# An encoder's last output rows: a spectrum's split moved into its step, the last product in two banks, the last store in quarters

## The chip, the cores and the metric

The kernel runs on one core of a Trainium2 chip. A core has a matrix engine (TensorE, PE in the profile; its weight loads are listed as PEld), a vector engine (VectorE, DVE), a scalar engine (ScalarE, ACT), GpSimd (POOL) and a sync engine (SyncE, SP) that issues transfers; transfers are also issued from the queues of ACT and POOL, and 16 DMA engines carry them all. Matrix products are accumulated in PSUM, in banks of 128 partitions by 512 fp32 columns; everything else on the chip lies in SBUF. The metric is the device time of one execution in microseconds (us), as the median of several runs.

## The reference: what is computed

Two sequences, of 2048 and of 512 positions with 1024 channels each, go through an encoder trunk of two layers and a final norm:

```
x = x + (banded_gqa(rmsnorm(x) @ w_in) * silu(gate)) @ w_out           # layer 0
h = rmsnorm(x)                                                          # layer 1
hg = h.reshape(b, s, 4, 256)
f = fft.fftn(hg, axes=(positions, group channels), norm="ortho").real
x = x + (f * silu(h @ w_gate)) @ w_fout
y = x * rsqrt(mean(x * x) + 1e-6) * final_norm                          # final RMSNorm
```

All is fp32. The two outputs are y of the two sequences. The change concerns the end of the second layer and the final norm of the last rows.

## The kernel before

**Precision.** An fp32 product is computed as three products in a faster format: each operand is split into a high part (a cast on ACT, `ACT.copy`) and a low part (the difference, a subtraction on DVE), and `matmul3` (lines 92 to 95) multiplies high by high, high by low and low by high. So each product of a 128-row tile with a K of 512 is 4 times 3 = 12 matmuls. Nearly all matmuls have line 95 in the profile and are told apart by their tiles.

**The Fourier layer.** The transform over 2048 positions is 16 by 128. Real and imaginary parts of the 16 "spectra" k1 are made by butterflies on DVE (`pm`, a sum and a difference of 128 by 1024 each, shown at line 1184); only k1 = 0 to 8 are transformed, since each k1 from 1 to 7 gives two tiles of 128 output rows, those of k1 and of 16 - k1. The function `position` (line 1330) transforms one spectrum: for each of two halves of the channels it takes the split operands (`halves_of`, lines 1316 to 1326: for the real and the imaginary part a cast on ACT at line 1323 and a subtraction on DVE at line 1324, 128 by 512 each), runs the products A and B on TensorE, and combines them on ACT and DVE (lines 1354 to 1361) into two tiles u, which are multiplied by the gates (line 1364). The split operands lie in tiles of the tag hT, of which there are eight.

**The output product.** `finish` (line 1384) multiplies u, turned, by the output weights and adds the residual rows, which `residual` loads from DRAM (line 1381). It then calls `normed` (line 1373): sum of squares on ACT (`sumsq`, line 979), the mean on DVE and the power of -1/2 on GpSimd (`inv_rms`, lines 86 to 90), one scaling of 128 by 1024 on DVE (line 1376) and a store issued from SP (line 1377). For the spectra 6, 1, 7, 3, 5 the class `Outs` (line 1397) takes the place of `finish`: both tiles of a spectrum are multiplied together, in seven products of 12 matmuls with sums of weights (T1, T2, T3, N4) and sums of operands (S1 to S4) instead of eight products. Its method `products` (line 1450) accumulates in the tiles W, Z and X, of which three banks (tag acc) serve, shared with the accumulators of `finish`; it adds each to the residual rows xa and xb with the function `add` (line 1457), and runs the next spectrum's `position` between its products.

**Around the sixth spectrum.** The tables T1, T2, T3, N4 (four loads of 512 KB each, line 1505) and many tiles of the butterflies share 16 buffers of the tag R. The real and imaginary parts of spectra 7, 3 and 5 are stored to DRAM (line 1656, issued from ACT) and read back later, which frees their buffers. The code first makes the butterflies up to g3r and g5r, then splits both halves of the sixth spectrum (line 1651), then makes the last butterfly (g5s and g3s, line 1652), then issues the six stores, then transforms the sixth spectrum with the operands made earlier.

**The tail.** In the last call of `products`, for spectrum 5, the last product (A[1, 1] with N4) goes into a bank of its own, Vo. The second half of the row's columns (512 to 1023) is complete before it, so its squares are summed early. After the product come the add, the square of columns 0 to 511, the sum of both, mean, power, and a scaling and a store for each half of the columns, one issued from SP and one from ACT.

**What sets the order.** Tile, the framework, plans the order of each engine's instructions: those that come first in the program go first where the plan finds them ready, by its own costs. An edge written with `after(ins, anchor)` fixes the order of two instructions of one engine. Each engine and each queue carries out its list in order; a load that needs a buffer waits at the head of its queue until the buffer's last reader or writer is done.

Of the kernel before, what the change touches and what calls it, by code (L numbers as in the profile page):

```python
# [9 lines left out]
F32 = mybir.dt.float32  # L10
# [9 lines left out]
P = 128  # L20
D = 1024
# [21 lines left out]
def encoder(  # L43
# [33 lines left out]
    def bank(name):  # L77
        return banks[-1].tile([P, 512], F32, tag="bank", name=name)
# [854 lines left out]
    def fourier_phase(tail):  # L933
        with ExitStack() as es:
# [15 lines left out]
            def zt(name):  # L950
                return right([P, D], F32, name)
# [27 lines left out]
            def sumsq(src, name):  # L979
                ss = main.tile([P, 8], F32, tag="ss", bufs=2, name=f"ss{name}")  # L980
                junk = fp.tile([P, 512], F32, tag="c12", bufs=1, name=f"jk{name}").bitcast(BF16)
                ACT.activation(junk, src, AF.Square, accum_out=ss[:, 0:1])
                return inv_rms(ss, 1, f"inv{name}")
# [413 lines left out]
            class Outs:  # L1397
# [52 lines left out]
                def products(self, hooks, last=False):  # L1450
# [25 lines left out]
                    normed(xa, self.us[0][1])  # L1476
                    prod(W, S[3], ft["T3"], four, False)
                    add(xb, 1, W)
                    if last:
                        ss = main.tile([P, 8], F32, tag="ss", bufs=2, name="ssl")  # L1480
                        junk = fp.tile([P, 512], F32, tag="c12", bufs=1, name="jkl").bitcast(BF16)
                        ACT.activation(junk[:, :512], xb[:, q[1]], AF.Square, accum_out=ss[:, 1:2])
                    if last:

                        add(xb, 0, W)
                        W = bank(f"Vo{self.n}")
                    prod(W, A[1, 1], ft["N4"], four, last)
                    add(xb, 0, W)
                    if not last:
                        normed(xb, self.us[1][1])  # L1490
                        return
                    ACT.activation(junk[:, :512], xb[:, q[0]], AF.Square, accum_out=ss[:, 0:1])
                    DVE.tensor_tensor(ss[:, 0:1], ss[:, 0:1], ss[:, 1:2], ALU.add)
                    inv = inv_rms(ss, 1, "invl")
                    for half in range(2):
                        hs = q[half]
                        DVE.scalar_tensor_tensor(xb[:, hs], xb[:, hs], inv[:, 0:1], gfb[:, hs], ALU.mult, ALU.mult)
                        (SP, ACT)[half].dma_start(out_rows(self.us[1][1])[:, hs], xb[:, hs])
# [152 lines left out]
            p6 = [halves_of("p6", *G[6], hf) for hf in range(2)]  # L1651
# [149 lines left out]
```

## Time and profile before

| | us |
|---|---|
| median of 3 runs | 1583.85 (1583.34 to 1585.53) |
| the profiled execution | 1584.07 |
| its span, first to last instruction | 1582.1 |
| TensorE busy in it | 1569.5 (99%) |
| VectorE busy in it | 1151.0 (73%) |
| mean TensorE clock granted | 0.999 of full speed |

A row of the timeline reads: start (us from the first instruction), duration, engine, line of the kernel, operation, output tile <- input tiles, shapes, and xN where N like ones in a row were merged; in brackets the idle time before it and what ended it. "PE W L95 x24" in the chain is a stretch of time with its start and length. A row of a group reads: line, engine, operation, tiles, shapes, count, then the busy time in us, the mean duration of one in ns, the idle time before them. A row of the DMA issues ends with the size in KB and the time from issue to landing in us. A row of the waits ends with the total in us, the number of waits and the longest. SPq and ACTq are the queues of SP and ACT.

### The profile page before, as it was taken

To read this page: it belongs to the slowest core of one execution; us is meant where nothing else is said; L and a number is where in the kernel's file an instruction comes from. 1 tells how busy PE (TensorE), PEld (TensorE's weight loads), DVE (VectorE), ACT (ScalarE), POOL (GpSimd) and SP (SyncE) were. 2 spreads that over 40 slices of the span, in tenths; PEclk is the share of its full clock that TensorE was granted. 3 is DMA by queue.
4 is the path that set the end of the run, shared out by engine and by line. 5 is a ranking of instruction groups with operands and counts; after the bars stand their busy time and mean duration, and the time that the engine had idled before them with its cause. 6 is when DMAs were issued, how large, how long until landed. Compare 5 with 4: busy or idle time off the path is not lost.

```text
span 1582.1 us, 27442 instructions
## 1 busy us (share of the span) xinstructions
PE 1569.5 (99%) x9743; PEld 1320.8 (83%) x9743; DVE 1151.0 (73%) x2785; ACT 874.5 (55%) x2089; POOL 446.5 (28%) x613
## 2 busy tenths in 40 slices
PE   9999999999999999999999999999999999999998
PEld 7888888888888888988888888888888888887886
DVE  6888656877447886378764577669778878988896
ACT  6688535776246784267752576646555554343342
POOL 2475642421404314024222242223112111011110
PEclk9999999999999999999999999999999999999999
DMA  7598695575856567655659566675567469548752
GB/s 293 200 332 290 227 359 210 207 262 201 295 205 224 205 234 276 216 215 214 257 165 329 208 221 232 236 262 196 196 207 258 175 223 410 183 167 318 264 203 80
DMA packets 101445, 373.89 MB, mean 236 GB/s; under 512 B 12236, under 2 KB 22476, under 8 KB 83901
## 3 DMA queue, kind: packets, MB, share of 16 engines
q1 hardware_dynamic: 82572, 297.91, 52.7%
q0 software_dynamic: 16400, 70.04, 11.4%
q10 hardware_dynamic: 2336, 4.20, 0.7%
q8 instruction: 77, 1.26, 0.3%
q14 instruction: 60, 0.48, 0.1%
HBM read 280.84 MB, written 91.26 MB: 235 GB/s over the span
## 4 chain that ended last, share of the span: by engine, by line
PE 95%; DVE 2%; DMA 1%; issue 0%; ACT 0%; POOL 0%; SPq 0%; DVEq 0%; POOLq 0%; ACTq 0%
PE gp L95 14%; PE qp L95 14%; PE spt L95 11%; PE op L95 7%; PE W L95 6%; PE av L557 6%; PE spt L472 6%; PE fo L95 5%; PE vp L95 3%; PE Z L95 3%; PE Wo L95 3%; PE pt L531 3%; PE Zo L95 2%; PE z L95 2%; PE X L95 2%; PE z L1079 1%
## 5 line engine op out<-in xcount | busy, mean ns | idle before, releaser
L95 PE MATMUL gp<-h,wg 128*128 128x512 f32 x960 | 237.6, 395 | 0.0
L95 PE MATMUL qp<-h,wq 128*128 128x512 f32 x960 | 237.3, 396 | 0.0
L491 DVE CUSTOM_DVE_ANT_0 S<-spt,b 128x385 f32<-128x385 f32 (+1 forms) x320 | 156.3, 527 | 105.1 <-PE spt L472 68.1
L95 PEld LDWEIGHTS gp<-h,wg 128*128 128x128 f32 x960 | 174.9, 188 | 37.2 <-issue 1.0
L95 PEld LDWEIGHTS qp<-h,wq 128*128 128x128 f32 x960 | 174.9, 188 | 36.7 <-issue 0.2
L499 ACT ACTIVATE S<-S 128x385 f32<-128x385 f32 (+1 forms) x320 | 188.8, 596 | 19.7 <-DVE S L491 19.5
L539 ACT CAST pts<-pt 128x384 fp32r<-128x384 f32 (+1 forms) x240 | 100.5, 457 | 168.2 <-PE pt L531 158.6
L540 DVE TENSOR_TENSOR pts<-pt,pts 128x384 fp32r<-128x384 f32 (+1 forms) x240 | 114.3, 519 | 23.3 <-ACT pts L539 22.2
L95 PE MATMUL spt<-wo,uT 128*128 128x512 f32 x480 | 120.4, 391 | 0.0
L581 POOL TENSOR_TENSOR uT<-o,uT 128x256 fp32r<-128x256 f32 x75 | 55.5, 739 | 229.3 <-ACT uT L580 229.2
L95 PE MATMUL op<-wo,uT 128*128 128x512 f32 x480 | 118.9, 391 | 0.0
L472 PE MATMUL spt<-kwin,qab 64*128 64x384 f32 (+1 forms) x960 | 118.4, 352 | 0.0
L557 PEld LDWEIGHTS av<-pts,v 128*128 128x128 f32 x576 | 101.4, 188 | 18.8
L95 PE MATMUL fo<-wo,tTu 128*128 128x512 f32 x480 | 115.7, 392 | 0.3 <-ACT wo L1556 0.3
L557 PE MATMUL av<-pts,v 128*128 128x512 f32 (+1 forms) x576 | 115.7, 341 | 0.0
L95 PEld LDWEIGHTS op<-wo,uT 128*128 128x128 f32 x480 | 89.3, 188 | 18.5
L95 PEld LDWEIGHTS spt<-wo,uT 128*128 128x128 f32 x480 | 89.1, 188 | 18.4
L95 PEld LDWEIGHTS fo<-wo,tTu 128*128 128x128 f32 x480 | 88.3, 188 | 17.6 <-ACT wo L1556 0.7
L511 DVE TENSOR_SCALAR S<-S 128x384 f32<-128x384 f32 (+1 forms) x192 | 96.0, 500 | 6.8
L472 PEld LDWEIGHTS spt<-kwin,qab 64*128 64x128 f32 x960 | 74.6, 186 | 28.2 <-issue 26.4
L577 POOL TENSOR_TENSOR o<-o,s 128x256 f32<-128x256 f32 x75 | 55.3, 737 | 135.1 <-DVE o L575 134.7
L531 PEld LDWEIGHTS pt<-ident,S 64*128 64x128 f32 x1328 | 78.4, 138 | 4.0 <-issue 1.8
(322 smaller groups left out, 3190.9 us busy)
## 6 DMA issues: line engine op xcount, KB each, us to landing
wo<-wsd SPq DMA_DIRECT2D x32, 1024.0 KB, 4.9
wq<-wsd SPq DMA_DIRECT2D x31, 1024.0 KB, 7.4
wg<-wsd SPq DMA_DIRECT2D x31, 1024.0 KB, 5.4
x<-x1d SPq DMA_DIRECT2D x40, 512.0 KB, 3.5
b<-b21d SPq DMA_DIRECT2D x40, 512.0 KB, 5.7
b<-rowd SPq DMA_DIRECT2D x40, 384.0 KB, 4.3
xs<-in_x_dram SPq DMA_DIRECT2D x23, 512.0 KB, 6.4
s2d<-gt POOLq DMA_DIRECT2D x40, 256.0 KB, 5.2
```

The costliest lines, as they stand in the source:

```text
L95: pe(PE.matmul(out, a[i], b[j], start=start and i + j == 0, stop=stop and i == 1, skip_group_check=more))
L472: pe(PE.matmul(banks[j][:, 2 + k0 * P : 2 + k1 * P], res["q"][rows, qp, b * P : (b + 1) * P], kwin[g][rows, kp, b * P + k0 * P : b * P + k ...
L491: seq(DVE, DVE.tensor_tensor_reduce(out=s[:, e0:e1], in0=ps[:, 1 + e0 : 1 + e1], in1=st["bias"][:, j, 386 - e1 : 386 - e0][:, ::-1], scale ...
L499: last_exp[0] = seq(ACT, ACT.activation(s[:, e0:e1], s[:, e0:e1], AF.Exp, bias=s[:, 386:387], scale=-1.0, accum_out=s[:, 387:388]))
L511: seq(DVE, DVE.tensor_scalar(s[:, ks], s[:, ks], den, None, ALU.mult))
L531: pe(PE.transpose(ps[h][:, kb, j, :], ss[j][rows, 1 + kb * P : 1 + (kb + 1) * P], ident[rows, rows]))
L539: seq(ACT, ACT.copy(hi, ps[:, k0:k1]))
L540: seq(DVE, DVE.tensor_tensor(lo, ps[:, k0:k1], f32(hi), ALU.subtract))
L557: pe(PE.matmul(to, v, pt, start=n == part == 0, stop=part == 1 and n in (1, len(todo) - 1), skip_group_check=n > 1,))
L577: eng.tensor_tensor(o, o, s, ALU.mult)
L581: low = eng.tensor_tensor(lo, o, f32(hi), ALU.subtract)
L1079: PE.matmul(to, m[part][:, g * P : (g + 1) * P], ch[:, 0, :, odd * P : (odd + 1) * P], start=part == 0, stop=part == 1,)
```

## The change

It has three parts. First, the second half of the sixth spectrum is no longer split ahead of the last butterfly; `position` splits it itself when it comes to its second half (it calls `halves_of` where it is given `None`).

Second, in the last call of `products`, the first rows xa are scaled in another way: DVE multiplies xa by the norm's weights gfb into a new tile ya, and when the inverse root is known, ACT scales ya and SP stores it. The mean's instruction on DVE is put behind the multiplication.

Third, the last product is done in two banks of 256 columns, each with 12 matmuls. The add and the square of columns 0 to 255 happen while the second bank is computed. DVE multiplies the finished columns by gfb into a tile yb in its free time: columns 512 to 1023 after the first bank, columns 0 to 255 after the second. The sum of squares comes in three parts; two are scaled and added ahead, and the third is added by the instruction that gives the mean. Then four quarters of 256 columns are scaled, three on DVE and one on ACT, and each is stored by itself, three from SP and one from ACT.

```diff
@@ -976,11 +976,11 @@
                         out.append((t[:, 0, k * P : (k + 1) * P], t[:, 1, k * P : (k + 1) * P]))
                 return out
-            def sumsq(src, name):
+            def sumsq(src, name, place=lambda ins: None):
                 ss = main.tile([P, 8], F32, tag="ss", bufs=2, name=f"ss{name}")
                 junk = fp.tile([P, 512], F32, tag="c12", bufs=1, name=f"jk{name}").bitcast(BF16)
                 ACT.activation(junk, src, AF.Square, accum_out=ss[:, 0:1])
-                return inv_rms(ss, 1, f"inv{name}")
+                return inv_rms(ss, 1, f"inv{name}", place)
@@ -1473,29 +1473,64 @@
                     prod(X, A[0, 1], wo[4:8], four, True)
                     add(xa, 0, X)
                     hooks[2]()
-                    normed(xa, self.us[0][1])
+                    if not last:
+                        normed(xa, self.us[0][1])
+                    else:
+
+                        ya, yb = zt("ya"), zt("yb")
+                        turned = DVE.tensor_tensor(ya, xa, gfb, ALU.mult)
+                        inv = sumsq(xa, "fa", lambda ins: after(ins, turned))
+                        scaled = ACT.activation(ya, ya, AF.Copy, scale=inv[:, 0:1])
+                        SP.dma_start(out_rows(self.us[0][1]), ya)
                     prod(W, S[3], ft["T3"], four, False)
                     add(xb, 1, W)
-                    if last:
-                        ss = main.tile([P, 8], F32, tag="ss", bufs=2, name="ssl")
-                        junk = fp.tile([P, 512], F32, tag="c12", bufs=1, name="jkl").bitcast(BF16)
-                        ACT.activation(junk[:, :512], xb[:, q[1]], AF.Square, accum_out=ss[:, 1:2])
-                    if last:
-
+                    if not last:
+                        prod(W, A[1, 1], ft["N4"], four, False)
                         add(xb, 0, W)
-                        W = bank(f"Vo{self.n}")
-                    prod(W, A[1, 1], ft["N4"], four, last)
-                    add(xb, 0, W)
-                    if not last:
                         normed(xb, self.us[1][1])
                         return
-                    ACT.activation(junk[:, :512], xb[:, q[0]], AF.Square, accum_out=ss[:, 0:1])
-                    DVE.tensor_tensor(ss[:, 0:1], ss[:, 0:1], ss[:, 1:2], ALU.add)
-                    inv = inv_rms(ss, 1, "invl")
+                    ss = main.tile([P, 8], F32, tag="ss", bufs=2, name="ssl")
+                    junk = fp.tile([P, 512], F32, tag="c12", bufs=1, name="jkl").bitcast(BF16)
+
+                    def square(cs, i):
+                        return ACT.activation(junk[:, cs], xb[:, cs], AF.Square, accum_out=ss[:, i : i + 1])
+
+                    def weigh(cs, prev):
+                        ins = DVE.tensor_tensor(yb[:, cs], xb[:, cs], gfb[:, cs], ALU.mult)
+                        after(ins, prev)
+                        return ins
+
+                    after(square(q[1], 0), scaled)
+                    add(xb, 0, W)
+                    prev = None
                     for half in range(2):
-                        hs = q[half]
-                        DVE.scalar_tensor_tensor(xb[:, hs], xb[:, hs], inv[:, 0:1], gfb[:, hs], ALU.mult, ALU.mult)
-                        (SP, ACT)[half].dma_start(out_rows(self.us[1][1])[:, hs], xb[:, hs])
+                        cs = slice(half * 256, half * 256 + 256)
+                        V = bank(f"Vo{half}")[:, :256]
+                        prod(V, A[1, 1], [(w[0][:, cs], w[1][:, cs]) for w in ft["N4"]], four, True)
+                        prev = DVE.tensor_tensor(xb[:, cs], xb[:, cs], V, ALU.add)
+                        square(cs, 1 + half)
+                        if not half:
+                            prev = weigh(q[1], prev)
+                            sums = DVE.tensor_scalar(ss[:, 0:1], ss[:, 0:1], 1.0 / D, EPS, ALU.mult, ALU.add)
+                            after(sums, prev)
+                        else:
+                            after(prev, sums)
+                    mean = DVE.scalar_tensor_tensor(ss[:, 1:2], ss[:, 1:2], 1.0 / D, ss[:, 0:1], ALU.mult, ALU.add)
+                    after(mean, prev)
+                    weigh(slice(0, 256), mean)
+                    inv = main.tile([P, 8], F32, tag="inv", bufs=2, name="invl")
+                    DVE.scalar_tensor_tensor(inv[:, 0:1], ss[:, 2:3], 1.0 / D, ss[:, 1:2], ALU.mult, ALU.add)
+                    POOL.tensor_tensor(inv[:, 0:1], inv[:, 0:1], mhalf[:, 0:1], ALU.pow)
+                    out = out_rows(self.us[1][1])
+                    for i, on_act in ((0, False), (3, True), (2, False), (1, False)):
+                        cs = slice(i * 256, i * 256 + 256)
+                        if on_act:
+                            ACT.activation(yb[:, cs], yb[:, cs], AF.Copy, scale=inv[:, 0:1])
+                        elif i == 1:
+                            DVE.scalar_tensor_tensor(yb[:, cs], xb[:, cs], inv[:, 0:1], gfb[:, cs], ALU.mult, ALU.mult)
+                        else:
+                            DVE.tensor_scalar(yb[:, cs], yb[:, cs], inv[:, 0:1], None, ALU.mult)
+                        (ACT if on_act else SP).dma_start(out[:, cs], yb[:, cs])
             ft = {w: [] for w in ("T1", "T2", "T3", "N4")}
@@ -1648,7 +1683,7 @@
             g1r, g7r = pm(e0c, o0c, "g1r")
             g1s, g7s = pm(o0s, e0s, "g1s")
             g3r, g5r = pm(e1c, o1s, "g3r")
-            p6 = [halves_of("p6", *G[6], hf) for hf in range(2)]
+            p6 = [halves_of("p6", *G[6], 0), None]
             g5s, g3s = pm(o1c, e1s, "g5s")
             G[1], G[7], G[3], G[5] = (g1r, g1s), (g7r, g7s), (g3r, g3s), (g5r, g5s)
             for k1 in (7, 3, 5):
```

## The prediction

> **What bounds the kernel.** I read the page first, then the waits of TensorE, then the order of instructions in two places: the last 10 us and the stretch from 1434 to 1462 us, which are the places the diff touches.
>
> ```profile
> span 1582.1 us, 27442 instructions
> PE 1569.5 (99%) x9743; PEld 1320.8 (83%) x9743; DVE 1151.0 (73%) x2785; ACT 874.5 (55%) x2089; POOL 446.5 (28%) x613
> PE 95%; DVE 2%; DMA 1%; issue 0%; ACT 0%; POOL 0%; SPq 0%; DVEq 0%; POOLq 0%; ACTq 0%
> 1495.10:1519.20 24.10, 24.10 (x125) 20.44 (x124) 21.18 (x37) 10.07 (x21) 4.06 (x4) 1.00 0.57 192
> PE Zo L95 <- issue: 1.4, 1, 1.4
> ```
>
> TensorE is busy for 99% and holds 95% of the chain. One of the last steps (1495 to 1519 us, the columns are PE, PEld, DVE, ACT, POOL busy) shows it without a gap: 24.10 of 24.10 us. So little can be won: TensorE idles 12.6 us in all (1582.1 - 1569.5), 7.45 of them behind its last matmul (which ends at 1571.77 + 2.88 = 1574.65, by the rows below), and 1.4 us in one stall, at the first product of the sixth spectrum that needs accumulator Z. The diff touches just these two places. Elsewhere I expect no difference.
>
> **The tail before.** The rows from the last product on:
>
> ```profile
> 1571.77 2.88 PE L95 MATMUL Vo<-fN,tT 128*128 128x512 f32 x12
> 1572.08 1.28 DVE L1376 SCALAR_TENSOR_TENSOR x<-x,invf,gfb 128x1024 f32<-128x1024 f32 x1 [0.73 <-POOL invf L89]
> 1573.29 1.28 DVE L1457 TENSOR_TENSOR x<-x,Wo 128x512 f32<-128x512 f32 x2
> 1574.05 0.63 ACT L1482 ACTIVATE jkl<-x 128x512 bf16<-128x512 f32 x1 [2.88 <-issue]
> 1574.69 0.69 DVE L1457 TENSOR_TENSOR x<-x,Vo 128x512 f32<-128x512 f32 x1
> 1575.47 0.63 ACT L1492 ACTIVATE jkl<-x 128x512 bf16<-128x512 f32 x1 [0.70 <-DVE x L1457]
> 1576.00 0.19 ACT L1492 ACTIVATION_READ_ACCUMULATOR jkl<-x 128x1 f32 x1
> 1576.22 0.16 DVE L1493 TENSOR_TENSOR ssl<-ssl 128x1 f32<-128x1 f32 x1 [0.85 <-ACT jkl L1492]
> 1576.42 0.15 DVE L88 TENSOR_SCALAR invl<-ssl 128x1 f32<-128x1 f32 x1
> 1576.71 0.55 POOL L89 TENSOR_TENSOR invl<-invl,mhalf 128x1 f32<-128x1 f32 x1 [4.67 <-DVE invl L88]
> 1577.30 1.42 DVE L1497 SCALAR_TENSOR_TENSOR x<-x,invl,gfb 128x512 f32<-128x512 f32 x2 [0.73 <-POOL invl L89]
> 1578.08 0.33 SPq L1498 DMA_DIRECT2D out_dram<-x  x1
> 1578.75 0.34 ACTq L1498 DMA_DIRECT2D out_dram<-x  x1
> out_dram<-x SPq DMA_DIRECT2D x1, 256.0 KB, 2.0
> ```
>
> Here every step waits for the one above it: add, square, its sum, mean, power, two scalings, two stores. The durations for the narrower pieces come from 256-wide instructions elsewhere in the same trace:
>
> ```profile
> 1115.71 2.87 PE z L95 x24
> 1118.59 2.75 PE W L95 x12
> L1360 DVE TENSOR_TENSOR up<-up,Bp 128x254 f32<-128x254 f32 x18 | 7.3, 411 | 0.0
> L1087 DVE SCALAR_TENSOR_TENSOR z<-z,z 128x256 f32<-128x256 f32 x40 | 14.4, 415 | 0.0
> L511 DVE TENSOR_SCALAR S<-S 128x256 f32<-128x256 f32 x24 | 10.9, 454 | 0.9
> L1354 ACT COPY up<-Ap 128x258 f32<-128x258 f32 x18 | 6.8, 377 | 26.5 <-PE Ap L95 20.6 <-DVE gp L1324 5.8
> 1478.54 1.75 SPq L1671 DMA_DIRECT2D go<-god  x4
> ```
>
> **The tail after, step by step.**
> (1) The product in two banks: 24 matmuls of 256 columns for 12 of 512. The two chain rows (24 narrow matmuls 2.87 us, 12 wide ones 2.75) price it at +0.12 us, the repeated weight loads in it. The last matmul ends near 1574.8.
> (2) The last add is 256 wide: 0.41 for 0.69, so 1574.8 to 1575.25; before it ended at 1575.38. Net of (1): 0.13 earlier. The other half's add runs under the second half's 1.43 us of matmuls.
> (3) The last square is 256 wide: about 0.40 for 0.63 (the 258-wide ACT copy's 0.377 is nearest), 0.23 earlier. The other two squares must be done by 1575.3. The first full-width rows' scaling goes from VectorE to ScalarE (1024 wide, about 1.1 us, starting near 1572.1 where L1376 stands now) and the square of columns 512 to 1023 is put behind it: 1573.2 to 1574.0, then the square of the first quarter pair to 1574.5. 0.8 us of room.
> (4) VectorE gets the product with gfb (1.2 us, 1570 to 1571.2, in its idle time before the power) in place of the 1.28 us of L1376, and gfb times columns 512 to 1023 (0.7 us) after the first half's add, near 1573.8 to 1574.5: idle time again. It also gets gfb times columns 0 to 255 (0.41), between the last add and the square's sum: 1575.25 to 1575.65, under the square. Cost nothing, while the square covers it; uncovered it would be 0.4.
> (5) L1493 and L88 (start to start 0.20, then 0.29 to the power) become one instruction: 0.20 earlier. So the power starts at 1576.71 - 0.13 - 0.23 - 0.20 = 1576.15 and ends at 1576.7.
> (6) Scaling by quarters: VectorE three (columns 0, 2, 1) and ScalarE one (3). Three rows of 0.41 to 0.45, which start about 0.35 to 0.4 apart, end near 1577.15, 1577.55 and 1577.95; before, the second half ended at 1578.72.
> (7) Stores: three on SP's queue, one on ACT's. The four 256 KB loads in 1.75 us give SP (1.75 - 0.33) / 3 = 0.47 us between issues (0.33 being one issue's own time in the rows above), so the issues are at 1577.2, 1577.65 and 1578.1: the queue, not VectorE, is the limit by a hair. The last issue moves from 1578.75 to 1578.1, 0.65 us earlier, and its transfer is 128 KB for 256.
>
> ```profile
> GB/s 0 473 382 437 419 455 164 0 0 0 0 36 0 0 0 0 0 0 0 0 0 64 400 391 319 364 410 364 18 0 0 0 0 0 0 0 0 0 0 0
> ```
>
> These slices (1574 to 1583 us, 0.225 us each) show the last two stores moving at about 380 GB/s from 1578.75 to 1580.3; so 128 KB less behind the last issue is 131 KB / 0.38 = 0.34 us. The first of the two landed at 1578.08 + 2.0 = 1580.1; what follows the last landing (to 1582.1) stays. Tail: -0.65 - 0.34 = **-1.0 us**. Bounds: -0.4 if the quarters' stores take as long as halves and SP issues 0.25 us slower each; -1.5 if scalings run at half the rows quoted.
>
> The Trainium skill, page "VectorE: DVE Perf Modes", section on the perf-mode tier table, says that an fp32 tensor_scalar within SBUF gives two results per cycle and a tensor_tensor one. By its figures a 256-wide one is an estimated 0.29 us, and the sum would be -1.1 only if SP's queue kept up; the row of L511 (0.454) does not show it. The same page's section on the errata says each SBUF-source instruction pays a fixed latency and advises 512 elements or more; that speaks against quarters. The rows agree in direction (two 254-wide adds 0.82 us, one 512-wide 0.69), and the sum above already holds it.
>
> **The sixth spectrum.** Four 512-wide splits stood ahead of the last butterfly (g5s, g3s); now two do, and the other two (a cast on ACT and a subtraction on VectorE each) come inside the step, between its halves.
>
> ```profile
> 1437.99 1.89 DVE L1324 TENSOR_TENSOR gp<-ev,gp 128x512 fp32r<-128x512 f32 x3
> 1441.05 0.33 ACTq L1656 DMA_DIRECT2D god<-g5s  x1
> 1443.65 0.41 DVE L1361 TENSOR_TENSOR up<-up,Bp 128x254 f32<-128x254 f32 x1
> 1445.69 0.42 DVE L1358 TENSOR_TENSOR up<-up,Bp 128x254 f32<-128x254 f32 x1 [0.55 <-PE Bp L95]
> 1449.93 1.28 DVE L1376 SCALAR_TENSOR_TENSOR x<-x,invf,gfb 128x1024 f32<-128x1024 f32 x1 [0.44 <-POOL invf L89]
> 1440.57 8.12 SPq L1505 DMA_DIRECT2D fT<-fT2d  x4
> 1451.25 0.34 SPq L1377 DMA_DIRECT2D out_dram<-x  x1
> 1451.64 1.41 SPq L1381 DMA_DIRECT2D x<-x1d  x3
> x<-x1d SPq DMA_DIRECT2D x1, 512.0 KB, 9.4
> 1461.11 1.28 DVE L1392 TENSOR_TENSOR x<-x,fo 128x512 f32<-128x512 f32 x2 [3.12 <-PE Wo L95]
> 1461.90 3.00 PE L95 MATMUL Zo<-fT,S 128*128 128x512 f32 x12 [1.37 <-issue]
> SPq L1505 <- DVE gp L1324: 0.7, 1, 0.7
> 1436.00:1462.00 26.00, 24.31 (x123) 20.12 (x123) 21.46 (x34) 8.72 (x18) 3.33 (x3) 1.00 0.98 373
> ```
>
> The 1.37 us stall is read backwards: Z needs an accumulator that the add of L1392 frees; that add starts at 1461.11, when the residual row lands (issued 1451.64 + 9.4 = 1461.0, which agrees to 0.1 us; the TensorE group that the row names wrote another accumulator). The load is slow because the DMA engines are 98% busy here, and it is issued behind the store of L1377, which waits for L1376, which stands behind the second half's L1361 by a written dependency.
>
> After: two subtractions (0.60 apart, so 1.2 us) leave the front, and g5s, g3s, their stores to memory and the first half's L1358 to L1361 each come up to 1.2 us earlier. Then the two subtractions and the second half's 12 matmuls of A (0.12 each, 1.4 us with B still to follow) stand between the first half's L1361 and the second half's L1358, where now 1445.69 - 1443.65 = 2.0 us pass. From 1443.65 - 1.2 = 1442.45: add 0.41, 1.2 and about 1.5 and L1358 starts near 1445.5, 0.2 earlier than before. TensorE meanwhile has the output products of earlier spectra to do. The bytes ahead of the residual row stay the same on engines that are full, so its landing moves little. I take **-0.2 us**. Bounds: -1.4 (the stall gone) and +2.9, worked out below. The sum is -1.0 - 0.2 = -1.2.
>
> **Rivals.**
> The stall goes as well: the earlier stores (g5s at 1439.9 for 1441.05) use DMA slack and free buffers earlier, the residual row lands 1.4 us sooner or more. For it: 1.2 us less ahead of the butterfly. Against: 98% DMA share. -1.0 - 1.4 = -2.4; with the smaller waits of the half and the tail's better end about -3.2.
> The other side: the T2 tables wait for buffers. SP's first T2 load waited 0.7 us for a split of the sixth spectrum (the L1505 row), since it takes over that buffer. With the second half's splits ending near 1443.7 in place of 1437.99 + 1.89 = 1439.9, that load is late by 3.8 us; the others, the store and the residual rows queue behind it on SP, and the stall becomes as much as 1.4 + 3.8. -1.0 + 3.8 = +2.8, or about +4 if second-half matmuls hold up L1376 too. Against: another buffer may serve, and between the end of the T2 issues (1440.57 + 8.12 = 1448.7) and the store's (1451.25) lie 2.6 us of room. It decides once the residual row lands over 1 us later; over 0.2% from 4.2 us on.
> The change does nothing: quarters' stores end together with the old halves, stall unchanged: -0.2.
>
> **How the numbers follow.** The profiled execution took 1584.07 us, 2.0 more than its span and 0.22 above the median of the three runs (1583.85). 1584.07 - 1.2 = 1582.9, which on the median is 1582.7. By cases: the forecast 0.47 (1582.7); stall gone 0.23 (1581.4, down to 1580.6); late tables 0.20 (1586.0, to 1588); nothing 0.10 (1583.7). The range is 1580.6 to 1586.2; the forecast's own is 1582.2 to 1583.6. A run of this kernel can be told from no change at about 0.2%, 3.2 us, and most cases stay inside: faster 0.14 (the far end of the second case and whatever the split saves that no row shows), slower 0.12 (the far end of the third), same 0.74.
>
> **What would show it.** In the new profile: Vo as two groups of 12 with about 3.0 us in all; the last square near 1575.3; the last store issue 1.6 us after the power ends and 3.4 us after the last matmul (now 4.1); the wait of Zo near 1.2 to 1.4 us. Wrong if: Zo's stall differs by over 1 us, a stall of TensorE appears between 1438 and 1470, SP issues the quarters over 0.6 us apart, or the last square waits for ScalarE's other work.

## The result, and the profile after

The changed kernel takes 1581.72 us (median of 22 runs, 1581.13 to 1584.42), the kernel before 1583.86 beside it (22 runs). The ratio is 0.9987 with a 95% interval of 0.9981 to 0.9993: 2.1 us (0.13%) less, inside the 0.2% that the prediction called "same" and inside its range (1580.6 to 1586.2), one microsecond under its 1582.7. The profiled execution took 1581.38 us against 1584.07, its span 2.7 us less.

The page of the kernel after: its span, the busy time of the engines and the chain by engine.

```profile
span 1579.4 us, 27477 instructions
PE 1569.0 (99%) x9755; PEld 1321.7 (84%) x9755; DVE 1153.0 (73%) x2790; ACT 876.5 (55%) x2093; POOL 446.1 (28%) x613
PE 96%; DVE 2%; ACT 1%; issue 0%; DMA 0%; POOL 0%; POOLq 0%; SPq 0%; DVEq 0%; ACTq 0%
```

TensorE's work is the same; its idle time fell from 12.6 to 10.4 us. The longest waits of TensorE (us in total, times, longest):

```profile
PE idle L242 <- DVE idle L239: 1.2, 1, 1.2
PE spt L95 <- ACT h L220: 1.0, 1, 1.0
PE trb L1015 <- DVE xrl L643: 0.3, 1, 0.3
```

The row that led this list before, Zo's 1.4 us, is gone. To see what each place gave, cut the two profiled executions at two matmuls: the first of Outs 6 (Wo, 1457.64 before, 1457.16 after) and the first of the last product (Vo, 1571.77 and 1569.68).

| stretch | before, us | after, us | difference |
|---|---|---|---|
| start to the first Wo of Outs 6 | 1457.64 | 1457.16 | -0.5 |
| from there to the first Vo | 114.13 | 112.52 | -1.6 |
| from there to the end of the span (the tail) | 10.3 | 9.7 | -0.6 |

The first row is no gain of the change: the last scaling at L1376 ahead of the split starts at 1435.15 instead of 1435.65 already, and in the kernels below this stretch lies between 1457.0 and 1458.2, whichever part of the change they hold (1458.17 with the tail alone, 1457.75 with the split alone). So the split part brought 1.6 us, for which I had 0.2, and the tail 0.6, for which I had 1.0.

**The sixth spectrum after.** The timeline of the kernel after, picked from 1438 to 1462 us:

```profile
1438.09 1.22 DVE L1184 TENSOR_TENSOR g5s<-tc,od 128x1024 f32<-128x1024 f32 x1
1439.11 0.32 SPq L1381 DMA_DIRECT2D x<-x1d  x1
1439.53 2.68 SPq L1540 DMA_DIRECT2D fT<-fT1d  x4
1442.30 6.60 SPq L1540 DMA_DIRECT2D fT<-fT2d  x4
1444.52 0.42 DVE L1358 TENSOR_TENSOR up<-up,Bp 128x254 f32<-128x254 f32 x1 [0.96 <-PE Bp L95]
1449.83 1.28 DVE L1376 SCALAR_TENSOR_TENSOR x<-x,invf,gfb 128x1024 f32<-128x1024 f32 x1 [0.73 <-POOL invf L89]
1451.14 0.34 SPq L1377 DMA_DIRECT2D out_dram<-x  x1
1451.57 0.86 SPq L1381 DMA_DIRECT2D x<-x1d  x2
1457.75 1.27 DVE L1392 TENSOR_TENSOR x<-x,fo 128x512 f32<-128x512 f32 x2
1459.88 2.88 PE L95 MATMUL Zo<-fT,S 128*128 128x512 f32 x12
```

DVE did what the change says: the butterfly g5s starts at 1438.09 instead of 1439.80. But the scaling at L1376 and the store at L1377 hardly moved (1449.93 to 1449.83, 1451.25 to 1451.14), so what follows the store on SP could not be earlier. The brackets say that the scaling waited for POOL's power in both kernels; the add at L1392 that this power comes from now starts behind L1361, at 1446.98 instead of 1444.46. What moved is one row of SP's queue. Before, all three loads of residual rows (x<-x1d) were issued from 1451.64 on, behind the eight tables and the store; after, one of them, the row that the add at L1392 waits for, is issued at 1439.11, ahead of all eight tables. The add starts at 1457.75, without a wait in its row, in place of 1461.11, and Zo follows Wo without a gap.

**The tail after.** The timeline of the kernel after, from the last product on:

```profile
1569.68 3.03 PE L95 MATMUL Vo<-fN,tT 128*128 128x256 f32 x24
1572.75 0.42 DVE L1510 TENSOR_TENSOR x<-x,Vo 128x256 f32<-128x256 f32 x1 [0.35 <-PE Vo L95]
1573.21 0.42 ACT L1496 ACTIVATE jkl<-x 128x256 bf16<-128x256 f32 x1 [0.93 <-DVE x L1510]
1573.53 0.19 ACT L1496 ACTIVATION_READ_ACCUMULATOR jkl<-x 128x1 f32 x1
1573.75 0.16 DVE L1522 SCALAR_TENSOR_TENSOR invl<-ssl 128x1 f32<-128x1 f32 x1 [0.17 <-ACT jkl L1496]
1574.05 0.55 POOL L1523 TENSOR_TENSOR invl<-invl,mhalf 128x1 f32<-128x1 f32 x1 [4.09 <-DVE invl L1522]
1574.64 0.62 DVE L1532 TENSOR_SCALAR yb<-yb,invl 128x256 f32<-128x256 f32 x2 [0.73 <-POOL invl L1523]
1575.02 1.31 SPq L1533 DMA_DIRECT2D out_dram<-yb  x3
1575.17 0.48 DVE L1530 SCALAR_TENSOR_TENSOR yb<-x,invl,gfb 128x256 f32<-128x256 f32 x1
```

From the first Vo to the power are 1574.05 - 1569.68 = 4.37 us, before 1576.71 - 1571.77 = 4.94. From the power to the end of the span are 5.35 us in both (1579.40 - 1574.05, 1582.06 - 1576.71). So all that the change did behind the power, the quarters and their stores, left the end where the power puts it. By the records of the transfers the last store landed 9.01 us after the first Vo before and 8.04 after, 0.97 earlier, and only 0.57 of that reached the end. Something else than the stores seems to end the kernel. The row that fits is the closing DRAIN on POOL's queue; whether it sets the end is tested further down. (A DRAIN is one of the instructions with which each queue closes the kernel. The row gives the shortest, median and longest duration in ns, then the first and last start.) In the kernel before:

```profile
L1796 POOLq DRAIN  x3: 46/97/4588, 1576.7 to 1581.8; - x3
```

and in the kernel after:

```profile
L1831 POOLq DRAIN  x3: 46/97/4592, 1574.0 to 1579.1; - x3
```

One of the three lasts 4.59 us and begins with the power, POOL's last work. It is over 8.94 us after the first Vo (before 9.51), and the end of the span is 0.78 later in both.

### The profile page after: what moved, and what is told of

Read it like the earlier page. It is cut to its first block, busy times and chain, and to the rows that moved or that the text cites. A ratio compares the mean times of both kernels' runs of the same rounds, so it can differ in the third digit from the quotient of the medians.

```text
span 1579.4 us, 27477 instructions
## 1 busy us (share of the span) xinstructions
PE 1569.0 (99%) x9755; PEld 1321.7 (84%) x9755; DVE 1153.0 (73%) x2790; ACT 876.5 (55%) x2093; POOL 446.1 (28%) x613
## 4 chain that ended last, share of the span: by engine, by line
PE 96%; DVE 2%; ACT 1%; issue 0%; DMA 0%; POOL 0%; POOLq 0%; SPq 0%; DVEq 0%; ACTq 0%
PE gp L95 14%; PE qp L95 14%; PE spt L95 11%; PE op L95 7%; PE W L95 6%; PE av L557 6%; PE spt L472 6%; PE fo L95 5%; PE vp L95 3%; PE Wo L95 3%; PE Z L95 3%; PE pt L531 3%; PE z L95 2%; PE Zo L95 2%; PE X L95 2%; PE z L1079 1%
## 5 line engine op out<-in xcount | busy, mean ns | idle before, releaser
L511 DVE TENSOR_SCALAR S<-S 128x384 f32<-128x384 f32 (+1 forms) x192 | 96.1, 501 | 6.8
```

Source lines behind the costliest of these rows:

```text
L511: seq(DVE, DVE.tensor_scalar(s[:, ks], s[:, ks], den, None, ALU.mult))
```

## Experiments on the sixth spectrum

Theory 1: the stall went because the residual row left the queue of tables on SP. Theory 2, my rival as I had it: the earlier butterfly and its earlier stores let the row land sooner. The tail alone, with both halves split ahead again:

```diff
-            p6 = [halves_of("p6", *G[6], 0), None]
+            p6 = [halves_of("p6", *G[6], hf) for hf in range(2)]
```

> The changed kernel with both halves of the sixth spectrum split ahead of the last butterfly again; only the tail is new. Both theories of the split expect the stall of Z's first product back, 1.2 to 1.6 us, and the second finish's residual row issued behind the tables again (near 1451.6 us). If parts add up, the tail alone is worth what its stretch in the two profiles shows (10.3 us from the last product's start to the span's end before, 9.7 after): 0.6 us, so a median near 1583.2. My prediction's figure for the tail, 1.0 us, would give 1582.9.

Measured: 1583.18 us, 0.9991 (0.9982 to 1.0000) of the kernel before. Its timeline:

```profile
1437.89 3.08 SPq L1540 DMA_DIRECT2D fT<-fT1d  x4
1452.17 1.46 SPq L1381 DMA_DIRECT2D x<-x1d  x3
1461.46 1.28 DVE L1392 TENSOR_TENSOR x<-x,fo 128x512 f32<-128x512 f32 x2 [2.93 <-PE Wo L95]
```

All three residual rows stand behind the tables again, and the waits have Zo back with 1.2 us. The tail is that of the kernel after, 9.7 us. The split alone, in the kernel before:

```diff
-            p6 = [halves_of("p6", *G[6], hf) for hf in range(2)]
+            p6 = [halves_of("p6", *G[6], 0), None]
```

> The kernel before with only the second half's split moved into the step; the old tail. Expected: no stall at Z, the residual row issued ahead of the T1 tables near 1439 us, the old tail of 10.3 us, and 1.4 to 1.6 us less than before: a median near 1582.4. If the two parts do not add, the median would lie within 0.5 us of 1583.85.

Measured: 1582.33 us, 0.9991 (0.9982 to 1.0000). One residual row is issued at 1439.63, Zo has no stall, the middle stretch is 112.49 us, and the tail stays at 10.3. By the profiles' stretches the two parts are independent, and each is worth what the table says. The times alone are too coarse to show that: this kernel and the last one have the same ratio and interval. Neither kernel separates the theories, since the split moves both the butterfly and the load. So the next one leaves the splits where they were before and asks for the residual rows ahead of the tables:

```diff
-            def finish(uT, r):
+            def finish(uT, r, x2=None):
                 r0 = r[0]
-                x2 = residual(r)
+                x2 = x2 or residual(r)
...
+            x2s = [residual(r) for uT, r in pend]
             f_sums("T1", right)
             f_sums("T2", right)
-            finish(*pend.pop(0))
+            finish(*pend.pop(0), x2s[0])
             o.operands()
-            finish(*pend.pop(0))
+            finish(*pend.pop(0), x2s[1])
```

> The kernel before, both halves of the spectrum split ahead of the butterfly as there, and only the residual row of the second finish loaded earlier in the program, ahead of the T1 and T2 tables. Theory 1 (the split's place matters only through the order of SP's queue, in which it lets the residual row pass the tables): the stall of 1.4 us goes although no split is moved; 1.3 to 1.6 us less than before, near 1582.4. Theory 2 (what counts is that 1.2 us of subtractions leave the front, so that the butterfly's stores go earlier and free buffers and transfer time): the stall stays at 1 us or more and the median within 0.5 us of 1583.85.

Measured: 1582.17 us, 0.9987 (0.9978 to 0.9996). Its timeline:

```profile
1437.31 0.39 SPq L1505 DMA_DIRECT2D fT<-fT1d  x1
1439.83 0.32 SPq L1381 DMA_DIRECT2D x<-x1d  x1
1440.24 1.56 SPq L1505 DMA_DIRECT2D fT<-fT1d  x3
1460.31 2.88 PE L95 MATMUL Zo<-fT,S 128*128 128x512 f32 x12
```

No split moved, the row is issued 12 us earlier, and the stall is gone: 112.49 us for the middle stretch, as with the split. Theory 1 holds, theory 2 is not needed. The other direction: the kernel after, with the load held behind the first finish's store.

```diff
                 after(DVE.scalar_tensor_tensor(x2, x2, inv[:, 0:1], gfb, ALU.mult, ALU.mult), last_b[0])
-                SP.dma_start(out_rows(r), x2)
+                return SP.dma_start(out_rows(r), x2)
...
-            def residual(r):
+            def residual(r, late=None):
                 x2 = x_tile(f"x2_{r[0]}")
-                SP.dma_start(x2, rows(x1d, r))
+                after(SP.dma_start(x2, rows(x1d, r)), late)
...
-                normed(x2, r)
+                return normed(x2, r)
...
-            finish(*pend.pop(0))
+            stored = finish(*pend.pop(0))
             o.operands()
-            finish(*pend.pop(0))
+            finish(*pend.pop(0), stored)
```

> The changed kernel, and only the residual row of the second finish put behind the store of the first finish's rows on SP's queue, where it stood before. Theory 1: the row is issued near 1451.5, lands near 1461, and Z stalls for 1.2 to 1.7 us again; median 1.3 to 1.6 us above the changed kernel's, near 1583.2. Theory 2: the stores and splits stand as in the changed kernel, so no stall and no difference from 1581.7 beyond 0.5 us.

Measured: 1585.77 us, 1.0006 (0.9996 to 1.0015), well above the 1583.2 expected. Two rows of SP's queue, and its waits of TensorE:

```profile
1437.45 3.15 SPq L1540 DMA_DIRECT2D fT<-fT1d  x4
1452.18 1.47 SPq L1381 DMA_DIRECT2D x<-x1d  x3
...
PE Ap L95 <- DVE gp L1324: 1.4, 2, 1.1
...
PE Zo L95 <- ACT gp L1323: 0.9, 1, 0.9
PE Ap L95 <- ACT gp L1323: 0.6, 1, 0.6
```

All three residual rows stand behind the tables again, and the stall at Zo came back with 0.9 us. The middle stretch is 3.8 us longer than after, and much of the rest went near 1489 us, where ACT waited for a spectrum that is read back from DRAM, and Ap for ACT and DVE:

```profile
1488.79 2.44 ACT L1323 CAST gp<-go 128x512 fp32r<-128x512 f32 x4 [3.02 <-DMA go<-god]
```

The added edge had changed the plan of the next step too: the four loads of that spectrum are issued behind a store on SP, at 1480.31, where the kernel after has them ahead of it, at 1476.44. So the direction of theory 1 is shown once more, its size is not measured by this kernel.

Why the plan puts the row ahead of the tables once the split is moved is not settled. That the first T1 load is issued 2.1 us later after the change (1439.53 for 1437.40) is not the reason; it follows from the new place of the row. SP's waits in the kernel after say so:

```profile
SPq L1381 <- DMA out_dram<-x: 2.3, 1, 2.3
```

The row stands first and waits 2.3 us at the head of SP's queue until the store of the rows before it has landed, and the tables wait behind it. In the kernel just shown, with the split in its new place but the row held back, the first T1 load is issued at 1437.45, as before the change.

## Experiments on the tail

First, the pieces ahead of the power. The last product in one bank of 512 columns, read in two halves:

```diff
+                    weigh(q[1], None)
+                    V2 = bank("Vo")
+                    prod(V2, A[1, 1], ft["N4"], four, True)
                     for half in range(2):
                         cs = slice(half * 256, half * 256 + 256)
-                        V = bank(f"Vo{half}")[:, :256]
-                        prod(V, A[1, 1], [(w[0][:, cs], w[1][:, cs]) for w in ft["N4"]], four, True)
-                        prev = DVE.tensor_tensor(xb[:, cs], xb[:, cs], V, ALU.add)
+                        prev = DVE.tensor_tensor(xb[:, cs], xb[:, cs], V2[:, cs], ALU.add)
                         square(cs, 1 + half)
                         if not half:
-                            prev = weigh(q[1], prev)
```

> The changed kernel with the last product in one bank of 512 columns (12 matmuls); add and square still go in two pieces of 256, and all else is as there. By my steps 1 to 3 the matmuls end 0.12 us earlier, but both adds and both squares come behind them: the power starts 0.3 to 0.6 us later than in the changed kernel and the tail is 0.2 to 0.6 us longer. If two banks are worth nothing: within 0.1 us.

Measured: 1581.84 us in one run (before: 1583.79). The power starts at 1574.49, 4.62 us after the first Vo instead of 4.37, and the tail is 10.0 instead of 9.7. Two banks are worth 0.25 us, a little under the 0.3 to 0.6 us that I had expected for the power. The first full-width rows scaled on DVE as before:

```diff
-                        ya, yb = zt("ya"), zt("yb")
-                        turned = DVE.tensor_tensor(ya, xa, gfb, ALU.mult)
-                        inv = sumsq(xa, "fa", lambda ins: after(ins, turned))
-                        scaled = ACT.activation(ya, ya, AF.Copy, scale=inv[:, 0:1])
-                        SP.dma_start(out_rows(self.us[0][1]), ya)
+                    normed(xa, self.us[0][1])
+                    if last:
+                        yb = zt("yb")
...
-                    after(square(q[1], 0), scaled)
+                    square(q[1], 0)
```

> The changed kernel with the other rows (xa) scaled in one instruction of 1.28 us on DVE and stored as before, instead of a multiplication on DVE ahead and a scaling on ACT. My step 4 priced ACT's part at nothing and its cover at the time in which DVE waits for the power. If that time counts, DVE's adds and the product with gfb start about 1.2 us later, run into the second bank's end, and the tail is 0.5 to 1.0 us longer; if the multiplication merely moved, within 0.1 us.

Measured: 1583.33 us in one run. The power starts 5.19 us after the first Vo, 0.82 later than after; the tail is 10.5. Its timeline shows why:

```profile
1571.01 1.28 DVE L1376 SCALAR_TENSOR_TENSOR x<-x,invf,gfb 128x1024 f32<-128x1024 f32 x1 [0.73 <-POOL invf L89]
1572.21 1.28 DVE L1457 TENSOR_TENSOR x<-x,Wo 128x512 f32<-128x512 f32 x2
1573.59 0.42 DVE L1504 TENSOR_TENSOR x<-x,Vo 128x256 f32<-128x256 f32 x1
1574.60 0.41 DVE L1504 TENSOR_TENSOR x<-x,Vo 128x256 f32<-128x256 f32 x1
```

The scaling holds DVE until 1572.3, both adds of Wo wait for it, and the first add of Vo starts 2.90 us after the first Vo (1573.59 - 1570.69), in the kernel after 1.64 (1571.32 - 1569.68). So the two banks pay only with this scaling off DVE; without that the tail would be worse than before (10.5 for 10.3).

Then the stores. The last quarter's store from ACT's queue instead of third on SP's:

```diff
-                        (ACT if on_act else SP).dma_start(out[:, cs], yb[:, cs])
+                        (ACT if i in (1, 3) else SP).dma_start(out[:, cs], yb[:, cs])
```

> The changed kernel with the last quarter's store (columns 256 to 511) issued from ACT's queue instead of SP's: two stores on each. In the changed kernel SP issues its three 0.49 us apart and the last one at 6.3 us after the last product's start, 0.35 us after its scaling ended. If SP's issues are the limit, the last issue comes at 6.0 us and the tail (last product's start to span's end, 9.7 us) shortens by 0.2 to 0.35 us; if the landing of the bytes is the limit, by less than 0.1.

Measured: 1581.13 us in one run, tail 9.71. The last issue came 0.25 us earlier (6.00 us after the first Vo for 6.24) and the last landing did not move (8.05 us after the first Vo, after: 8.04). Two stores of 256 KB instead of four of 128:

```diff
-                    for i, on_act in ((0, False), (3, True), (2, False), (1, False)):
+                    for i, on_act in ((0, False), (3, True), (1, False), (2, False)):
...
-                        (ACT if on_act else SP).dma_start(out[:, cs], yb[:, cs])
+                        if i in (1, 2):
+                            hs = q[i // 2]
+                            (SP, ACT)[i // 2].dma_start(out[:, hs], yb[:, hs])
```

> The changed kernel with the same four scalings, but two stores of 256 KB (one from SP after columns 0 to 511, one from ACT after columns 512 to 1023) instead of four of 128 KB. If the smaller last transfer is worth the 0.34 us that I gave it, and the issue on SP costs 0.3, the tail stays at 9.7 us; if the size of the last transfer is worth nothing, the tail is 0.3 us shorter than the changed kernel's, since both issues come at 5.8 to 6.0 us from the last product's start.

Measured: 1581.52 us in one run, tail 9.71. The last landing came 0.3 us later (8.36), and the end stood still. That is the first sign that the stores don't set the end. My next thought was the closing work of SP, which goes through a list of waits and drains after the last landing; two kernels made that list end earlier. In the first, the store of the rows ya is issued from POOL:

```diff
-                        SP.dma_start(out_rows(self.us[0][1]), ya)
+                        POOL.dma_start(out_rows(self.us[0][1]), ya)
```

> The changed kernel with one edit: the store of the other rows (ya, 512 KB), issued 1.5 us after the last product's start, goes out from POOL's queue and not from SP's. Theory: SP ends the kernel with a fixed list of waits, two semaphores each and 0.06 us apart; the transfers of SP and ACT take eight semaphores in turn, and in the changed kernel the last store has the one that stands second in the list, so that nine more steps (0.5 us) follow its landing, where before two did. One transfer fewer on SP shifts the turn by one, the last store then has a semaphore near the list's end: the landing stays at 8.0 us from the last product's start, the end comes 1.2 to 1.3 us behind it (now 1.68), the tail is 9.3 us for 9.7 and the median 0.3 to 0.5 us under the changed kernel's 1581.7. Rival: the end follows the landing by a time that the transfers set themselves; then the tail stays at 9.7.

Measured: 1581.79 us, 0.9987 (0.9978 to 0.9996); landing 8.05, SP's list done at 8.19 instead of 8.6, and the end at 9.81, later than after (POOL, which now has a store of its own to issue, drains for 4.69 us instead of 4.59). In the second, three last stores instead of four, two quarters together from ACT:

```diff
-                        (ACT if on_act else SP).dma_start(out[:, cs], yb[:, cs])
+                        if i == 2:
+                            ACT.dma_start(out[:, q[1]], yb[:, q[1]])
+                        elif not on_act:
+                            SP.dma_start(out[:, cs], yb[:, cs])
```

> The changed kernel with three last stores in place of four: columns 0 to 255 and 256 to 511 from SP, 512 to 1023 in one from ACT, behind the same four scalings. It shifts the turn of the semaphores by one too, without another queue. If the list of waits is what counts: the first store still goes at 5.3 us from the last product's start, the bytes are the same, the landing is at 8.0 to 8.2, the end 1.2 to 1.3 us behind it, the tail 9.3 to 9.45 us for 9.7. If the transfers themselves set the end: 9.7 or more.

Measured: 1581.12 us, 0.9980 (0.9971 to 0.9989); SP's list done at 8.17, the end at 9.72. The closing list falls as a reason too. What was left was POOL's drain. It can be moved both ways. Later, by a multiplication on POOL that reads the last quarter and whose result is not used:

```diff
                         (ACT if on_act else SP).dma_start(out[:, cs], yb[:, cs])
+                    POOL.tensor_tensor(ss[:, 3:4], inv[:, 0:1], yb[:, 256:257], ALU.mult)
```

> The kernel after the change, with one small multiplication added on POOL (128x1) that reads the last scaled quarter and whose result nobody uses; the stores are as they were. Theory (POOL's closing drain sets the end: it starts with POOL's last work, lasts 4.59 us in the kernels before and after, and the end comes 5.35 us behind the start of that work): the last work on POOL now starts about 6.1 us after the first matmul of the last product instead of 4.4, so the end comes 10.9 to 11.4 us after it instead of 9.7, and the kernel is 1.2 to 1.7 us slower than after (about 1583.2). Rival (the end hangs on the landing of the last store, 8.0 us after the first matmul, and on what the engines do behind it; the drain only fills the time): the stores are not touched, so the end stays at 9.7 and the time at about 1581.7.

Measured: 1583.13 us, 0.9995 (0.9986 to 1.0004), tail 11.1. Its timeline and the closing line's group:

```profile
1576.04 0.19 POOL L1534 TENSOR_TENSOR ssl<-invl,yb 128x1 f32<-128x1 f32 x1 [1.21 <-DVE yb L1530]
...
L1832 POOLq DRAIN  x3: 46/97/4230, 1576.0 to 1580.8; - x3
```

The stores land at 8.04 as before, and the end is 1.4 us later: the drain now begins 6.1 us after the first Vo. And earlier, by taking the power off POOL in the kernel with three stores (a square root of a small tile, which POOL makes from xa, has ACT's root table loaded some 15 us earlier, when ACT has nothing to do):

```diff
                     add(xa, 1, Z)
+                    if last:
+                        one = main.tile([P, 8], F32, tag="one", bufs=1, name="one")
+                        POOL.tensor_tensor(one, xa[:, 512:520], xa[:, 512:520], ALU.mult)
+                        ACT.activation(one, one, AF.Sqrt)
...
-                    POOL.tensor_tensor(inv[:, 0:1], inv[:, 0:1], mhalf[:, 0:1], ALU.pow)
+                    ACT.activation(inv[:, 0:1], inv[:, 0:1], AF.Sqrt)
+                    DVE.reciprocal(inv[:, 0:1], inv[:, 0:1])
```

> The kernel with three last stores, and the last power taken off POOL: ACT takes a square root (128x1, its table loaded some 9 us earlier, behind the second-last sum of squares, where ACT is idle) and DVE the reciprocal. POOL's last work is then the power for the first half of the rows, about 0.2 us before the first matmul of the last product. Theory (the drain sets the end): its 4.59 us are over about 4.5 us after that matmul, the end falls back to the landing of the last store (8.0, give or take 0.2 for the other way to the inverse root) with SP's closing steps (8.2) and the 0.7 us that follow: 8.8 to 9.2 instead of 9.7, time about 1580.5, ratio to before 0.9977 to 0.998. Rival (the end hangs on the landing by a fixed 1.7 us): 9.5 to 9.9, and the time stays at about 1581.1 to 1581.5.

Measured: 1580.37 us, 0.9976 (0.9967 to 0.9985), tail 8.7. Its timeline and the closing line's group:

```profile
1559.89 1.28 ACT L1475 ACT_TABLE_LOAD   x1
1574.63 0.20 ACT L1527 ACTIVATE invl<-invl 128x1 f32<-128x1 f32 x1 [0.23 <-DVE invl L1526]
1574.87 0.16 DVE L1528 RECIPROCAL invl<-invl 128x1 f32<-128x1 f32 x1 [0.27 <-ACT invl L1527]
1575.07 0.62 DVE L1537 TENSOR_SCALAR yb<-yb,invl 128x256 f32<-128x256 f32 x2
...
L1839 POOLq DRAIN  x3: 46/97/4588, 1570.1 to 1578.8; - x3
```

The drain begins with the power of the rows before (1570.11) and is over long before the stores. The end falls by 1.05 us against the kernel with three stores and the power on POOL. The shorter way to the inverse root brought the last landing from 8.03 to 7.76, 0.27 earlier; the rest, 0.78, is time that the drain had held. The end now follows the landing by 0.9 us, and SP's closing list, done at 7.90, outlasts POOL's drain. In one table, in us after the first Vo:

| kernel | last work on POOL starts | drain over | last store landed | end |
|---|---|---|---|---|
| before | 4.95 | 9.51 | 9.01 | 10.29 |
| after | 4.37 | 8.94 | 8.04 | 9.72 |
| last quarter by ACT | 4.37 | 8.93 | 8.05 | 9.71 |
| halves stored | 4.37 | 8.93 | 8.36 | 9.71 |
| one bank | 4.63 | 9.19 | 8.30 | 9.97 |
| rows on DVE | 5.19 | 9.76 | 8.86 | 10.54 |
| rows' store by POOL | 4.38 | 9.03 | 8.05 | 9.81 |
| three stores | 4.37 | 8.93 | 8.03 | 9.72 |
| POOL late | 6.13 | 10.34 | 8.04 | 11.12 |
| three stores, root on ACT | -0.27 | 4.29 | 7.76 | 8.67 |

In every row but the last the end is the drain's end + 0.78. The last kernel is the fastest of all by its tail. Against before it gains 3.6 us; beside the kernel after it was not run, and the two ratios' intervals (0.9967 to 0.9985, 0.9981 to 0.9993) overlap a little, so the profile's 1.05 us is the better measure of that step.

## Why the prediction was right, and where it was not

The total came out inside the range, 0.5 us below the forecast's own (1582.2 to 1583.6), and not by the forecast's mechanism: what happened is the first rival, "the stall goes as well" (chance 0.23, 1581.4 us), by a road that I had not described. By the prediction's own list it was wrong there: "Zo's stall differs by over 1 us" came true. That the total fits is luck as far as the mechanism goes: one term was too small, the other too large, and the range was wide enough for what was left.

**The sixth spectrum, -0.2 forecast, -1.6 measured.** The step that failed is "the bytes ahead of the residual row stay the same on engines that are full, so its landing moves little". It took SP's list of transfers as given. The plan made a new list, and eight tables that had stood ahead of the row stood behind it. DVE's times, the step before it, were 1.0 us off at the second half's L1358 (I had it at 1445.5, 0.2 earlier than before, and it came at 1444.52), but the store at L1377, on which the row would have waited, moved by only 0.1. The lower bound of this term (-1.4, the stall gone) was passed by 0.2. My reason for the rival, stores and buffers that come free earlier, fell with the third kernel: the stall goes with no split moved.

**The other side, T2 tables that wait 3.8 us longer, did not happen.** The first T2 load was issued at 1442.30 instead of 1440.57, 1.7 us later, and the last one's issue ended nearly as before (1448.9 for 1448.7). The store behind them was issued at 1451.14, 2.2 us after that, so this lateness held nothing up. The rival rested on a row that I had read wrongly: the wait of 0.7 us for L1324 lies between 1438.6 and 1440.4, where SP issued the last two T1 loads, and not at the first T2 load. Its sum doesn't come out either: +2.8 on 1583.85 is 1586.65 and not 1586.0, and the +2.9 that I gave as the bound is nowhere worked out.

**Steps 1 to 5, the way to the power: right.** I had 0.13 + 0.23 + 0.20 = 0.56 us; measured 0.57. The 24 matmuls took 3.03 us for 2.88 (0.15, forecast 0.12), and from the square's start to the next instruction of DVE 0.54 us passed for 0.75 (0.21 less, forecast 0.23). The cover of step 4 held: the product with gfb ran under the square. Moving the other rows' scaling off DVE, which step 4 gave no worth of its own, is what the rest needs: without it the power starts 0.82 us later.

**Steps 6 and 7, quarters and stores: the right number for the landing by luck, and worth nothing at the end.** SP's three issues started 0.45 us apart on average ((1575.9 - 1575.0) / 2; forecast 0.47) and the landing came 0.97 earlier (forecast 1.0). But I had added this up from the last issue, 0.65 earlier, and a last transfer half as large, 0.34, and the runs bear out neither: an issue 0.25 earlier of the last quarter left the landing where it was, and with halves it came 0.3 later, where my terms (their last issue 0.2 earlier, their last transfer 0.34 longer) give 0.14. What the landing goes with is the first issue: it comes 2.64 to 2.71 us behind it in every kernel of the table (6.31 to 9.01 before, 5.34 to 8.04 after, 5.72 to 8.36 with halves), and the first issue is 0.97 earlier. So the number agreed, but not for my reasons. My sign "1.6 us after the power ends" for the last issue was a slip; by my steps it was 1.4 (1578.1 - 1576.7), and it came at 1.3.

The size of the tail's term failed at "what follows the last landing (to 1582.1) stays": what followed was no fixed piece but POOL's drain, which the power starts. So the tail gave 0.57 us, the part of the power, and the 0.4 us of the stores fell off the path. I had also put three quarters on DVE at 0.41 to 0.45; the two TENSOR_SCALAR took 0.35 each and started 0.27 apart (0.62 together). Nothing came of it, since SP's issues and then the drain stood above it. The prediction's estimate of 0.29 us from the Trainium skill, page "VectorE: DVE Perf Modes", section on the perf-mode tier table, was nearer to this than the row of L511 (0.454) which I preferred.

**The rival "nothing"** failed on both counts: the stall went, and the last landing came earlier; only that the stores gave the end nothing was as it had it, for another reason.

In the sum 1.4 us too little was given to the split and 0.4 too much to the tail: -1.2 forecast, -2.2 in these two stretches, -2.1 between the medians.

## What to carry to other kernels

When a planner orders the queues, a change in one engine's work can reorder a transfer on a queue that the diff never names: for each stall near a change, ask which transfer it waits for, what stands ahead of that on its queue, and whether the plan still puts it there; a load that is wanted soon is better asked for ahead of the long ones than left to the plan. For the end of a kernel, don't follow only the data: list for each engine its last work and what closes behind it, since the end comes with the latest of these, and a tiny last instruction on the wrong engine can cost more than the last store.

## What the runs showed of the hardware

POOL's closing drain takes 4.59 us from the start of a last power of 128x1 (0.55 us itself), and 4.23 from the start of a last multiplication of 128x1 (0.19): about 4.0 us behind POOL's last work in both, with the last stores in two, three or four pieces; with a store on POOL's own queue it took 0.1 us more (4.69). The end of the execution follows it by 0.78 us. In the kernel whose POOL ends early, the end follows the last landing by 0.91 us.

Half a megabyte of stores takes about 1.5 us from its first byte to its last, in four pieces, three or two (7.69 - 6.17, 7.66 - 6.17, 8.01 - 6.56 us after the first Vo): in the kernels of the table the last landing came 2.64 to 2.71 us behind the first issue, and an earlier last issue gained nothing. No kernel moved the first issue alone.
